# Memory operands made by ScalarE and VectorE in the neighbourhood slots instead of by GpSimd in the grouped-query ones, and fill in pieces half as long

## The chip, the cores and the metric

The kernel runs on one core of a Trainium2 chip. The metric is device time in microseconds (us) of one launch. The engines are TensorE (PE; PEld is its weight load), VectorE (DVE), ScalarE (ACT), GpSimd (POOL) and SyncE (SP), which issues nearly all DMAs. Each engine runs its instructions in the order in which the built program has them, and waits at the head of that order.

## What is computed

Two layers of an encoder over 512 tokens of width 1024, all in f32, and a final norm. One layer of the reference, cut to what matters:

```
x += W_out [ NA(h) || GQA(h) ]              h = RMSNorm(x), one input projection w_in
     NA : 8 heads, 2-D neighbourhood attention on an 8 x 64 grid, window 8 x 16, learned bias
     GQA: 8 query heads on 2 key/value heads, q and k normalised per head and rotated, 512 keys
x += MemoryCrossAttention(RMSNorm(x), RMSNorm(mem))     4 heads over 256 memory tokens
x += ConvFFN(RMSNorm(x))                    SwiGLU with a width-3 depthwise convolution

def memory_cross_attention(h, mem_n, w_q, w_kv, w_o):
    q  = (h @ w_q).reshape(b, s, MEM_HEADS, MEM_HEAD_DIM)
    kv = (mem_n @ w_kv).reshape(b, m, 2, MEM_HEADS, MEM_HEAD_DIM)
    ...
```

mem_n is RMSNorm(mem) times a gain per layer (norm_mem_kv). Its statistic does not depend on the layer; the gain does.

## The kernel before, in words

**Operands in two halves.** To keep f32 accuracy every operand of a large matmul is a pair: hi, the value cast to a shorter format (fp32r), and lo, the remainder. A product is three matmuls (mm3, L353). For weights, emit_split (L255) makes the pair: ScalarE casts (L271), GpSimd subtracts (L272). At most two raw weights and four pairs are held (N_RAW, N_W).

**Two attentions woven with filler.** In each layer the attention runs as two calls of weave (L163). The first has 8 neighbourhood units (two heads, half of the queries), the second 16 grouped-query units (two heads, a block of 128 queries). A slot of weave runs one stage of each of several units: the scores of unit s (na_scores L738, gqa_scores L907), the softmax normalisation of unit s-1 (normalise, L489, mostly on GpSimd: L490), the transposes of the probabilities of unit s-2 (na_transpose L778, gqa_transpose_p L932), and the product with the values. After a transpose, ScalarE casts the PSUM result (L483) and VectorE subtracts (L484), and only then is the PSUM buffer free. Scores use two PSUM buffers (sc), transposes and small statistics two (tr), everything else four (mm). The scores' buffers come free when ScalarE has taken the exponentials (L763, L921).

Between the stages TensorE gets other work from a Filler (L127): a chain of generators (projections of q, k, v, of the grouped-query heads, then the output projection, the memory keys and values) that yield after each piece. A Filler is asked for so many nanoseconds of matmuls (NA_FILL three times per neighbourhood slot, GQA_FILL once per grouped-query slot); it runs whole pieces until it has given them, and what it gave too much is taken off the next request. A piece is mostly 12 matmuls of 512 columns, 2.7 us. N_FIRST pieces run ahead of the first slot.

**Work that comes due later.** Late (L101) holds functions until TensorE has been given so many more LATE (3600 ns) of matmuls: late(2, double) doubles a key, late(2, straddle) copies the V blocks that straddle two tiles. The rotation of a grouped-query head is such a chain (gqa_rope, L855): swap copies (four small DMAs t<-t), a power on GpSimd (L879, 1.65 us) and a spread (L880), an addition (L884), four small matmuls with the identity ("rows"), and a split (L700, L702). PE and SP keep the program's order. For ScalarE, VectorE and GpSimd a scheduler fixes the order when the program is built, by a priority that follows the program's order; behind(n) (L193) shifts it back by n, or forward where n is negative.

**The memory operands.** memory_prepare (L523) loads mem (two DMAs of 512 KB into two r tiles) and makes, for each of 8 chunks of 128x256: a multiplication by the gain on GpSimd (L535), a cast on ScalarE (L536), a subtraction on GpSimd (L537). It is stepped in the grouped-query slots by MEM_STEPS, and the memory keys need it near the end of that stage (memory_keys, L1016). mem_stat (L545) forms the statistic once, in layer 0; its last step copies mem_rep out of a tr buffer (L570).

**Tiles.** The pool r has 22 buffers of 4 KB per partition for nearly everything in pairs, t has 12 of 2 KB for temporaries.

Of the kernel before, what the change touches and what calls it, by code (L numbers as in the profile page):

```python
# [12 lines left out]
AF = mybir.ActivationFunctionType  # L13
# [14 lines left out]
MEMN = 256  # L28
# [15 lines left out]

GQA_ORDER = ["k", 0, 1, "v", 2, 3]


NA_FILL = 2500
GQA_FILL = [2300] * 16 + [4300, 3600, 3000, 3000]
MEM_FILL = [1, 1, 2, 2, 1, 3, 1, 3, 1, 3, 1]  # L50
N_ROWS = 3
MEM_STEPS = [0, 0, 1, 0, 1, 1, 1, 1, 1, 1, 1] + [0] * 9
LATE = 3600
W_BEHIND, N_RAW, N_W, AHEAD, AHEAD_HELD, N_WARM, N_LATE, N_FIRST = 45, 2, 4, 2, 5, 8, 4, 4


class InOrder:
# [119 lines left out]
def encoder_kernel(ctx: ExitStack, tc: tile.TileContext, t: dict, out: bass.AP):  # L177
# [6 lines left out]
    cpool = ctx.enter_context(tc.tile_pool(name="cpool", bufs=1))  # L184
    xpool = ctx.enter_context(tc.tile_pool(name="xpool", bufs=1))
    wpool = ctx.enter_context(tc.tile_pool(name="wpool", bufs=N_W))
    rpool = ctx.enter_context(tc.tile_pool(name="rpool", bufs=22))
    tpool = ctx.enter_context(tc.tile_pool(name="tpool", bufs=12))
    spool = ctx.enter_context(tc.tile_pool(name="spool", bufs=24))
    psum = ctx.enter_context(tc.tile_pool(name="psum", bufs=2, space=PSUM))  # L190

# [331 lines left out]
    def memory_prepare(l):  # L523

        mops.clear()
        raw = load_mem()
        yield
        yield
        for c in range(KC):
            if c % 2 == 0:  # L530
                mg = rtile((2, 2, MEMN))
            g = par[:, l, G_MKV + c : G_MKV + c + 1]
            hi, lo = mg[:, 0, c % 2, :], mg[:, 1, c % 2, :]
            src = raw[c // 4][:, c % 4, :]
            POOL.tensor_scalar(src, src, g, 1.0, op0=ALU.mult, op1=ALU.mult)  # L535
            ACT.copy(hi, src)  # L536
            POOL.tensor_sub(lo, src, f(hi))  # L537
            mops.append((hi, lo))
            if c % 2 == 1:
                yield  # L540
# [4 lines left out]
    def mem_stat():  # L545

        acc = None
        for i in range(KC // 2):
            sq = tmp((2, MEMN))
            SP.dma_start(sq, t["memT"][i * 256 : (i + 1) * 256, :].rearrange("(k p) n -> p k n", p=P))  # L550
            yield
            ACT.activation(sq, sq, AF.Square)
            if acc is None:
                acc = sq
            else:
                POOL.tensor_add(acc, acc, sq)
        POOL.tensor_add(acc[:, 0], acc[:, 0], acc[:, 1])
        yield
        pv = ps_t()
        for b in range(MB):  # L560
            PE.matmul(pv[:, b : b + 1], acc[:, 0, b * P : (b + 1) * P], ones, start=True, stop=True)
        v = small(MB)
        DVE.tensor_scalar(v, pv[:, 0:MB], 1.0 / D, EPS, op0=ALU.mult, op1=ALU.add)
        POOL.tensor_tensor(mem_rstd, v, mhalf[:, :MB], op=ALU.pow)
        yield
        pr = ps_t()
        for b in range(MB):
            PE.matmul(pr[:, b * P : (b + 1) * P], mem_rstd[:, b : b + 1].to_broadcast([P, P]), ident,
                      start=True, stop=True)
        ACT.copy(mem_rep, pr[:, :MEMN])  # L570
        yield


# [32 lines left out]
    for l in range(DEPTH):  # L606
# [42 lines left out]
        def project_qk(n, p):  # L649
            w = get_w((n, p))  # L650
            pm = ps_mm() if p else ps_s()
            gemm_T(pm, w, xg, range(0, 4), 0, KC - 1)
            yield
            gemm_T(pm, w, xg, range(4, 8), 0, KC - 1)
            if (n, p) == ("q", 0):
                mix.stat()
                held.append(pm)
            elif (n, p) == ("k", 0):
                mix.spread()
                split_qk("q", 0, held.pop())  # L660
                split_qk("k", 0, pm)
            else:
                split_qk(n, p, pm)
            yield
# [41 lines left out]
        def project_v(g):  # L706

            w = [get_w(("v", g, kh)) for kh in range(2)]
            vs = [rtile((2, 4, P)) for _ in range(4)]
            vblk[g] = {P * b: vs[b // 2][:, b % 2] for b in range(NB)}  # L710
            vblk[g].update({P * b + 64: vs[2 + b // 2][:, b % 2] for b in range(NB - 1)})
            for b in range(NB):
                pm = ps_mm()[:, :256]
                bs = slice(b * P, b * P + P)
                for k in range(KC):
                    wh, wl = (v[:, k % 4, :] for v in w[k // 4])
                    mm3(pm, xg[k][0][:, bs], xg[k][1][:, bs], wh, wl, k == 0, k == KC - 1)
                v = vblk[g][P * b]
                split_psum(v[:, :, 0:HD], v[:, :, HD:P], pm.rearrange("p (h d) -> p h d", d=HD), mix.rstd[:, b : b + 1])
                if b == NB - 1:  # L720
                    late(2, lambda: straddle(vs))
                yield

        def straddle(vs):
# [104 lines left out]
        def gqa_project(g):  # L829
            w = get_w(("g", g))  # L830
            pm = ps_mm()
            for h in range(2):
                gemm_T(pm, w, xg, range(4 * h, 4 * h + 4), 0, KC - 1)
                if h == 0:
                    yield
            if g == "v":
                gqa_v(pm)
            else:
                gqa_rope(g, pm)
            yield  # L840
# [139 lines left out]
        def close_rows(n, ops, ready, norm, between):  # L980


            w, rows = [], []
            yield lambda: ready(1)
            for m in range(n):
                if m % 2 == 0:
                    w.append(get_w(("outg", 0, m // 2)))
                rows.append((ps_mm(), w[m // 2], slice(P * (m % 2), P * (m % 2) + P)))
                gemm_T(*rows[m][:2], ops, range(2), 0, 3, rows[m][2])
                yield  # L990
            next(between)
            yield
            yield lambda: ready(2)
            for pm, ws, c in rows:
                gemm_T(pm, ws, ops, [2], 0, 3, c)
            yield lambda: ready(3)
            yield from between
            norm = norm()

            def begin(m):  # L1000
                if m // 2 == len(w):
                    w.append(get_w(("outg", 0, m // 2)))
                rows.append((ps_mm(), w[m // 2], slice(P * (m % 2), P * (m % 2) + P)))
                gemm_T(*rows[m][:2], ops, range(3), 0, 3, rows[m][2])

            begin(n)
            for m in range(KC):
                if m == len(rows):
                    begin(m)
                pm, ws, c = rows[m]  # L1010
                gemm_T(pm, ws, ops, [3], 0, 3, c)
                norm.close(m, pm)
# [3 lines left out]
        def memory_keys():  # L1016
            yield lambda: len(mops) == KC
            for h in range(4):
                if h % 2 == 0:
                    kt = rtile((2, 2, MEMN))  # L1020
                    memk.extend((kt[:, i, 0, :], kt[:, i, 1, :]) for i in range(2))
                pm = ps_mm()[:, :MEMN]
                gemm_T(pm, get_w(("memk", h)), mops, range(KC), 0, KC - 1)
                u = tmp((MEMN,))
                DVE.tensor_mul(u, pm, mem_rep)
                ACT.copy(memk[h][0], u)
                DVE.tensor_sub(memk[h][1], u, f(memk[h][0]))
                yield

        def memory_values(g):  # L1030
# [3 lines left out]
            for b in range(MB):  # L1034
                pm = ps_mm()[:, :256]
                bs = slice(b * P, b * P + P)
                for k in range(KC):
                    wh, wl = (v[:, k % 4, :] for v in w[k // 4])
                    mm3(pm, mops[k][0][:, bs], mops[k][1][:, bs], wh, wl, k == 0, k == KC - 1)
                c = slice(256 * g, 256 * g + 256)  # L1040
                split_psum(memv[b][0][:, c], memv[b][1][:, c], pm, mem_rstd[:, b : b + 1])
                yield

        if l > 0:
# [5 lines left out]
            out_na(), memory_keys(), memory_values(0),  # L1050
            close_rows(2, PartsView(parts, 4), lambda k: whole[k], lambda: nns.append(Norm(G_MQ, l)) or nns[0],
                       memory_values(1)))
        attn_fill.step(N_FIRST if l == 0 else N_FIRST + 4)

        stat = Filler(PE, late, mem_stat()) if l == 0 else None

        def na_quanta(s):
            if l == 0 and s < 7:
                stat.step(1)
            if s == 3:  # L1060
                gtab.append(rtile((2, S), F32))
                SP.dma_start(gtab[0], t["rope"])
# [1 line left out]
            return [NA_FILL] * 3  # L1064

        weave(8, [(2, na_transpose), None, (1, na_normalise), (0, na_scores), None, (2, na_values), None], attn_fill.run, na_quanta)
        ms = Filler(PE, late, memory_prepare(l))

        def gqa_quanta(s):
            ms.step(MEM_STEPS[s])  # L1070
            return [GQA_FILL[s]]

        weave(4 * NB, [(2, gqa_transpose_p), (1, gqa_normalise), (0, gqa_scores), (3, lambda u: gqa_values(u, 0)),
                       (4, lambda u: gqa_values(u, 1)), None], attn_fill.run, gqa_quanta)
        attn_fill.finish()
        nn = nns[0]

# [328 lines left out]
```

## Time and profile before

| | |
|---|---|
| Runs | 1377.2, 1378.24, 1379.76 us; median 1378.24 |
| The profiled execution | 1377.65 us; its span 1375.1 us |
| Instructions in the span | 19228 |
| Layer 0, both attentions | about 20 to 230 us of the span: PE busy 203.87 of 210 |
| Layer 0, memory attention and FFN | 230 to 690: PE busy 458.31 of 460 |
| Layer 1, both attentions | 690 to 905: PE busy 209.09 of 215 |
| Layer 1, memory attention, FFN and end | 905 to 1375: PE busy 460.22 of 470 |
| GpSimd on the memory operands | L535 16 x 0.478 us, L537 16 x 0.742 us (median) |
| ScalarE on the memory operands | L536 16 x 0.406 us (mean) |

How to read the profile: a row of a timeline is the start, the time to the end of the last of its instructions, the engine, the line in the kernel, the operation, the tiles out<-in, the shapes and how many instructions were merged. In brackets stands how long the engine had been idle and whose work ended the wait. In a table by stretch, each engine has its busy time and its number of instructions; behind them stand the granted clock, the share of the DMA engines and GB/s. A matmul's end is modelled and reaches into the next, so PE's busy time fills some gaps.

### The profile page before, as it was taken

What the parts mean: (1) busy time and instruction counts of PE and PEld (TensorE: products, weight loads), DVE (VectorE), ACT (ScalarE), POOL (GpSimd) and SP (SyncE); (2) the same over time, 40 slices, a digit from 0 to 9 for tenths busy, and PEclk for the clock granted to TensorE, in tenths of its full rate; (3) what the DMA queues carried; (4) which work ended last, traced back from release to release, by engine and by line L of the source; (5) the groups of instructions that cost most, each with busy time, mean ns of one, the idle gap of its engine ahead of it and who ended that gap; (6) DMA issues with size and microseconds to landing.
All of it is one profiled execution on the core that took longest, in us unless ns stands there. A gap on an engine that the chain in (4) does not pass through costs nothing.

```text
span 1375.1 us, 19228 instructions
## 1 busy us (share of the span) xinstructions
PE 1348.7 (98%) x7072; PEld 1152.6 (84%) x7072; DVE 861.8 (63%) x1520; ACT 674.5 (49%) x1256; POOL 706.5 (51%) x525
## 2 busy tenths in 40 slices
PE   9999999999999999999999989999999999999997
PEld 7898789888888888888888978998788888888897
DVE  6666775565886188268546567745758834861874
ACT  6765676554543243233457657755554422432441
POOL 2557865626444443443645677657264444444441
PEclk9999999999999999999999999999999999999999
DMA  6753322222333333332266441233143333333331
GB/s 213 226 157 86 89 58 78 89 65 79 106 92 99 100 92 91 108 93 88 81 184 179 128 127 36 62 93 92 32 122 92 93 107 92 95 89 108 95 90 62
DMA packets 219293, 139.87 MB, mean 102 GB/s; under 512 B 6080, under 2 KB 212160, under 8 KB 219200
## 3 DMA queue, kind: packets, MB, share of 16 engines
q1 hardware_dynamic: 219056, 138.65, 34.4%
q8 instruction: 56, 0.92, 0.3%
q14 instruction: 37, 0.30, 0.1%
q10 hardware_dynamic: 144, 0.00, 0.0%
HBM read 126.05 MB, written 2.10 MB: 93 GB/s over the span
## 4 chain that ended last, share of the span: by engine, by line
PE 84%; DVE 5%; ACT 4%; POOL 3%; DMA 2%; issue 1%; SPq 0%; DVEq 0%; ACTq 0%; POOLq 0%
PE mm L78 75%; PE sc L78 5%; PE tr L65 3%; POOL lo L272 2%; PE tr L78 1%; ACT hi L271 1%; DVE mm L435 1%; DVE xT L436 1%; ACT t L763 1%; DMA raw<-in_w_mem_q 1%; DMA raw<-in_w_mem_o 0%; SPq L65 0%; DVE r L702 0%; DMA raw<-in_w_in 0%; ACT r L700 0%
## 5 line engine op out<-in xcount | busy, mean ns | idle before, releaser
L272 POOL TENSOR_TENSOR lo<-raw,hi 128x1024 fp32r<-128x1024 f32 (+2 forms) x268 | 498.9, 1872 | 469.8 <-ACT hi L271 467.3
L78 PE MATMUL mm<-xg,hi 128*128 128x512 f32 x1920 | 594.4, 391 | 0.7 <-ACT t L863 0.7
L78 PEld LDWEIGHTS mm<-xg,hi 128*128 128x128 f32 x1920 | 356.8, 188 | 72.6 <-ACT t L863 0.9
L271 ACT CAST hi<-raw 128x512 fp32r<-128x512 f32 (+2 forms) x276 | 224.2, 836 | 337.1 <-PE mm L78 274.7
L78 PE MATMUL mm<-xg,lo 128*128 128x512 f32 x960 | 373.8, 389 | 0.0
L78 PE MATMUL mm<-r,hi 128*128 128x512 f32 (+1 forms) x1144 | 331.5, 374 | 1.9 <-DVE xg L449 1.6
L78 PEld LDWEIGHTS mm<-r,hi 128*128 128x128 f32 x1144 | 207.0, 189 | 40.3 <-DVE xg L449 3.2
L1230 DVE SCALAR_TENSOR_TENSOR t<-t,par,t 128x7 f32<-128x7 f32 (+1 forms) x352 | 201.8, 640 | 34.0 <-ACT t L1223 34.0
L78 PE MATMUL mm<-r,lo 128*128 128x512 f32 (+1 forms) x572 | 212.9, 372 | 0.0
L78 PEld LDWEIGHTS mm<-xg,lo 128*128 128x128 f32 x960 | 180.2, 188 | 37.9
L78 PEld LDWEIGHTS mm<-r,lo 128*128 128x128 f32 x572 | 107.8, 188 | 18.7
L1215 DVE TENSOR_TENSOR t<-mm,rep 128x512 f32<-128x512 f32 x88 | 60.1, 687 | 78.2 <-PE mm L78 62.5
L490 POOL TENSOR_SCALAR t<-t,s 128x512 f32<-128x512 f32 (+1 forms) x112 | 66.7, 611 | 67.8 <-DVE s L769 32.6
L1236 DVE TENSOR_TENSOR r<-t,r 128x512 fp32r<-128x512 f32 x44 | 90.4, 2054 | 7.3 <-ACT r L1235 4.1
L1232 ACT ACTIVATE t<-t 128x512 f32<-128x512 f32 x44 | 27.9, 633 | 134.3 <-DVE t L1230 134.3
L1259 DVE TENSOR_TENSOR xT<-xT,mm 128x512 f32<-128x512 f32 x32 | 21.9, 685 | 106.8 <-PE mm L78 106.8
L65 PE MATMUL tr<-ident,t 128*128 128x128 f32 x456 | 63.0, 274 | 10.6 <-POOL t L490 4.1
L78 PE MATMUL sc<-r,r 128*128 128x256 f32 (+1 forms) x352 | 70.8, 334 | 1.8 <-ACT t L921 1.8
L65 PEld LDWEIGHTS tr<-ident,t 128*128 128x128 f32 x456 | 52.1, 141 | 21.2 <-issue 4.5
L1223 ACT ACTIVATE t<-t,par 128x512 f32<-128x512 f32 x88 | 66.8, 806 | 3.3 <-DVE t L1215 3.3
L78 PE MATMUL mm<-r,r 128*128 128x256 f32 (+1 forms) x428 | 62.6, 298 | 0.1
L78 PEld LDWEIGHTS mm<-r,r 128*128 128x128 f32 x428 | 56.1, 191 | 2.8 <-DMA r<-r 0.3
(151 smaller groups left out, 1572.0 us busy)
## 6 DMA issues: line engine op xcount, KB each, us to landing
raw<-in_w_up SPq DMA_DIRECT2D x88, 512.0 KB, 3.7
raw<-in_w_in SPq DMA_DIRECT2D x33, 512.0 KB, 4.3
raw<-in_w_down SPq DMA_DIRECT2D x32, 448.0 KB, 3.7
raw<-in_w_mem_kv SPq DMA_DIRECT2D x16, 512.0 KB, 3.8
raw<-in_w_down SPq DMA_DIRECT2D x16, 512.0 KB, 4.0
r<-in_bias SPq DMA_DIRECT2D x16, 384.0 KB, 5.5
r<-r SPq DMA_DIRECT2D x22, 256.0 KB, 4.9
raw<-in_w_out SPq DMA_DIRECT2D x8, 512.0 KB, 3.6
```

The costliest lines, as they stand in the source:

```text
L65: return lambda *a, **k: self.tc.keep_in_program_order(op(*a, **k))
L78: return self.tc.keep_in_program_order(self.engine.matmul(out, lhsT, rhs, **k))
L271: act.copy(hi[:, k], raw[:, k])
L272: (POOL if eng[0] == "P" else DVE).tensor_sub(lo[:, k], raw[:, k], f(hi)[:, k])
L435: DVE.tensor_add(pm, pm, xT[c])
L490: eng.tensor_scalar(e, e, sums[:, col : col + 1], 1.0, op0=ALU.mult, op1=ALU.mult)
L1215: DVE.tensor_mul(u, us[side], ffn.rep)
L1223: ACT.activation(cc, u, AF.Identity, bias=par[:, l, CB + ch : CB + ch + 1], scale=w[1])
L1230: DVE.scalar_tensor_tensor(cc[:, dst], u[:, src], wi, cc[:, dst], op0=ALU.mult, op1=ALU.add)
L1232: ACT.activation(cs[0], cs[0], AF.Silu)
L1236: DVE.tensor_sub(acts[j][1], cs[0], f(acts[j][0]))
L1259: DVE.tensor_add(xT[m], xT[m], pm)
```

## The change

- memory_prepare is stepped in the neighbourhood slots from slot 5 on, one step a slot, in place of the grouped-query slots; its second empty yield is gone. A chunk is now a copy with the gain as a scale on ScalarE (hi) and one scalar_tensor_tensor on VectorE, src x gain - hi (lo), both put back by 40 in the scheduler's order. GpSimd has no part in it.
- The pieces of the filler are halved: projections yield after two chunks of the contraction in place of four (6 matmuls of 512 columns), V blocks and memory values after four in place of eight, memory keys after four. N_FIRST becomes 7 and 16 (4 and 8 whole pieces before). close_rows takes two half pieces where it took one.
- NA_FILL goes from 2500 to 2550; straddle is due one LATE earlier; the copy of mem_rep is moved forward by 30.
- The pool r has 21 buffers, t 14.

```
-NA_FILL = 2500
+NA_FILL = 2550
-MEM_STEPS = [0, 0, 1, 0, 1, 1, 1, 1, 1, 1, 1] + [0] * 9
-W_BEHIND, N_RAW, N_W, AHEAD, AHEAD_HELD, N_WARM, N_LATE, N_FIRST = 45, 2, 4, 2, 5, 8, 4, 4
+W_BEHIND, N_RAW, N_W, AHEAD, AHEAD_HELD, N_WARM, N_LATE, N_FIRST = 45, 2, 4, 2, 5, 8, 4, (7, 16)
...
-    rpool = ctx.enter_context(tc.tile_pool(name="rpool", bufs=22))
-    tpool = ctx.enter_context(tc.tile_pool(name="tpool", bufs=12))
+    rpool = ctx.enter_context(tc.tile_pool(name="rpool", bufs=21))
+    tpool = ctx.enter_context(tc.tile_pool(name="tpool", bufs=14))
...
         raw = load_mem()
         yield
-        yield
         for c in range(KC):
...
-            POOL.tensor_scalar(src, src, g, 1.0, op0=ALU.mult, op1=ALU.mult)
-            ACT.copy(hi, src)
-            POOL.tensor_sub(lo, src, f(hi))
+            with behind(40):
+                ACT.activation(hi, src, AF.Copy, scale=g)
+                DVE.scalar_tensor_tensor(lo, src, g, f(hi), op0=ALU.mult, op1=ALU.subtract)
...
-        ACT.copy(mem_rep, pr[:, :MEMN])
+        with behind(-30):
+            ACT.copy(mem_rep, pr[:, :MEMN])
...
         def project_qk(n, p):
             w = get_w((n, p))
             pm = ps_mm() if p else ps_s()
-            gemm_T(pm, w, xg, range(0, 4), 0, KC - 1)
-            yield
-            gemm_T(pm, w, xg, range(4, 8), 0, KC - 1)
+            for k in range(0, KC, 2):
+                gemm_T(pm, w, xg, range(k, k + 2), 0, KC - 1)
+                if k + 2 < KC:
+                    yield
...
                     mm3(pm, xg[k][0][:, bs], xg[k][1][:, bs], wh, wl, k == 0, k == KC - 1)
+                    if k == 3:
+                        yield
...
-                    late(2, lambda: straddle(vs))
+                    late(1, lambda: straddle(vs))
...
-            for h in range(2):
-                gemm_T(pm, w, xg, range(4 * h, 4 * h + 4), 0, KC - 1)
-                if h == 0:
+            for k in range(0, KC, 2):
+                gemm_T(pm, w, xg, range(k, k + 2), 0, KC - 1)
+                if k + 2 < KC:
                     yield
...
-            next(between)
-            yield
+            for _ in range(2):
+                next(between)
+                yield
...
-                gemm_T(pm, get_w(("memk", h)), mops, range(KC), 0, KC - 1)
+                w = get_w(("memk", h))
+                gemm_T(pm, w, mops, range(0, 4), 0, KC - 1)
+                yield
+                gemm_T(pm, w, mops, range(4, 8), 0, KC - 1)
...
-        attn_fill.step(N_FIRST if l == 0 else N_FIRST + 4)
+        attn_fill.step(N_FIRST[l])
+        prepare = Filler(PE, late, memory_prepare(l))
...
         def na_quanta(s):
             if l == 0 and s < 7:
                 stat.step(1)
+            if s >= 5:
+                prepare.step(1)
...
-        ms = Filler(PE, late, memory_prepare(l))
-        def gqa_quanta(s):
-            ms.step(MEM_STEPS[s])
-            return [GQA_FILL[s]]
         weave(4 * NB, [(2, gqa_transpose_p), (1, gqa_normalise), (0, gqa_scores), (3, lambda u: gqa_values(u, 0)),
-                       (4, lambda u: gqa_values(u, 1)), None], attn_fill.run, gqa_quanta)
+                       (4, lambda u: gqa_values(u, 1)), None], attn_fill.run, lambda s: [GQA_FILL[s]])
```

More of the change, by code (lines that the diff above doesn't have):

```diff
@@ L1039, in memory_values @@
                     mm3(pm, mops[k][0][:, bs], mops[k][1][:, bs], wh, wl, k == 0, k == KC - 1)
+                    if k == 3:
+                        yield
                 c = slice(256 * g, 256 * g + 256)
```

## Prediction

> **What bounds the kernel now.** I read the page first, then busy time by stretch, then what TensorE waited for, then the engines around those waits.
>
> ```profile
> PE 1348.7 (98%) x7072; PEld 1152.6 (84%) x7072; DVE 861.8 (63%) x1520; ACT 674.5 (49%) x1256; POOL 706.5 (51%) x525
> ...
> PE   9999999999999999999999989999999999999997
> ...
> PE 84%; DVE 5%; ACT 4%; POOL 3%; DMA 2%; issue 1%; SPq 0%; DVEq 0%; ACTq 0%; POOLq 0%
> ```
>
> TensorE (PE) bounds it. The change adds and removes no matmul, so only PE's gaps can shrink. Where they are, by stretch (length, then busy time of PE, PEld, DVE, ACT, POOL):
>
> ```profile
> 60.00:145.00 85.00, 83.55 (x524) 74.52 (x523) 54.37 (x136) 53.64 (x133) 54.70 (x56) 1.00 0.46 131
> 145.00:175.00 30.00, 26.82 (x156) 22.08 (x156) 22.42 (x42) 22.06 (x52) 26.25 (x36) 1.00 0.33 98
> ...
> 690.00:808.00 118.00, 117.88 (x726) 105.36 (x725) 68.14 (x171) 71.37 (x172) 65.03 (x68) 1.00 0.51 152
> 808.00:832.00 24.00, 18.97 (x107) 15.29 (x106) 14.34 (x28) 13.08 (x28) 18.05 (x23) 1.00 0.48 139
> ```
>
> The neighbourhood stretches (60 to 145, 690 to 808) lose little; the openings of grouped-query attention (145 to 175, 808 to 832) lose 3.2 and 5.0 us, and GpSimd (POOL) is the busiest engine beside PE in the first. Busy time hides part of a gap, since matmuls overlap, so I size gaps from one matmul's start to the next, less the usual step (227 ns for 512 columns). Over 0.15 us, in layer 0: 0.36 at 85.6, 0.68 at 97.6, 0.90 at 117.1, 1.01 and 0.17 at 149 to 151, 1.79 at 159.1, 0.86 at 172.1, 0.82 and 1.00 at 218 to 220; together 7.6. In layer 1: 0.52 at 775, 1.97 at 817.7, 2.51 at 822.3, 0.17 at 825.4, 1.03 at 829.6, 0.93 at 850.8; together 7.1. So 14.7 us is the ceiling of the gain.
>
> The largest, by GpSimd's and by TensorE's instructions in order of time:
>
> ```profile
> 818.60 1.27 POOL L272 TENSOR_TENSOR lo<-raw,hi 128x512 fp32r<-128x512 f32 x1 [0.37 <-ACT hi L271]
> 819.84 1.39 POOL L535 TENSOR_SCALAR r<-r,par 128x256 f32<-128x256 f32 x3
> 821.19 1.30 POOL L272 TENSOR_TENSOR lo<-raw,hi 128x512 fp32r<-128x512 f32 x1
> 822.46 1.84 POOL L535 TENSOR_SCALAR r<-r,par 128x256 f32<-128x256 f32 x4
> 824.27 1.36 POOL L490 TENSOR_SCALAR t<-t,s 128x512 f32<-128x512 f32 x2
> ```
> ```profile
> 819.89 1.40 PE L78 MATMUL sc<-r,r 128*128 128x512 f32 x4 [1.80 <-ACT t L921]
> ...
> 825.02 1.21 PE L65 MATMUL tr<-ident,t 128*128 128x128 f32 x7 [2.35 <-POOL t L490]
> ```
>
> Seven memory multiplications (L535) stand in GpSimd's queue ahead of the softmax normalisation (L490) that the transposes need. In layer 0 the memory's casts (L536) do the same on ScalarE (ACT): they hold back the copy (L483) that frees a transpose buffer, at 159.1.
>
> ```profile
> 157.50 1.33 ACT L536 CAST r<-r 128x256 fp32r<-128x256 f32 x4
> 158.85 1.07 ACT L483 CAST xg<-tr 128x512 fp32r<-128x512 f32 x2
> ```
>
> **The change, part by part.** The order in which the built program's instructions stand on each engine is the same before and after outside the two attention stages: start, memory attention and FFN cost nothing either way, though the pools change size (r 22 to 21, t 12 to 14).
>
> GpSimd loses 16 x 0.478 (L535) and 16 x 0.742 (L537), 19.5 us. ScalarE swaps 16 casts of 0.406 for 16 scaled copies; L775, the same shape with a scale, takes 0.512, so +1.7 us. VectorE (DVE) gains 16 instructions of two SBUF operands; from L1025 with one PSUM operand (0.425) to that plus the rest of a GpSimd subtraction (L272, 1.30), so 0.43 to 1.7 each. The nearest row is L1027 (same shape, two SBUF operands): 0.415 to 0.976, median 0.818. I take 0.82, 13 us in both layers. They and the copies stand in neighbourhood slots 5 to 9, some 48 us per layer, where VectorE is 64% busy; 6.6 more make 0.78, about its share at 145 to 175 (0.75). The two memory loads go ahead of weight loads on SP's queue one slot group earlier; SP sits on its own waits there (12.8 us at 65.4), and the copies come 7 to 10 us of matmuls after the loads, which took 6.1 us to land: nothing. The wait added: the copies sit in ScalarE's in-order queue behind that load, with softmax exponentials behind them.
>
> Layer 1, opening (5.7 us of gaps). In the new order GpSimd has L272 x2 (already run at 809.0 to 811.6), then L512, L884, L879, L880, then the normalisation. From the split of the last NA output at 813.4: 1.29 + 1.29 + 1.65 + 0.61 gives 818.3, the first half normalised by 819.0; the pieces before the first transposes end at 820.2, so no wait. The first exponentials no longer stand behind ScalarE's weight cast (which caused the 1.97): 816.1 and 816.8, just before the second scores at 816.4 and 816.8. The next transposes wait for VectorE to empty their buffers behind two score maxima (0.65 each): 0.4 for the first half, 0.4 for the second, behind L977 and L873. They end at 825.9, where the trace has 831.4: **5.5 gained**. The gap at 850.8 (0.93) is a rope's split (L702 twice, 1.39) ahead of a transpose copy, with 4.1 us between transposes; there the spacing becomes 5.4 and it goes, but the previous rope's spacing falls from 5.4 to 4.1 and by the same sum gets 1.1: 0.2 lost. The wait at 775 is for a copied V block whose copy is now issued one LATE step (3.6 us of PE) earlier: 0.4 gained.
>
> Layer 0, opening (2.97 of gaps). The first transposes wait behind L879 (1.65) at 148.1, which now stands after the normalisation: 1.2 gone. L536 gone from ScalarE: 1.8 gone. But ScalarE's new order has the copies of the first transposes ahead of the second pair of exponentials (before, behind them), and the third scores need those exponentials' buffers. From the trace's own steps, transposes' start to copy 0.69, two copies 1.25, one exponential 0.70: 2.7 after their start, where 0.87 would do: 1.8 lost, and 0.5 at the fifth scores in the same way. What is late next is that. **0.7 gained.** At 172 the transposes stand one half piece (1.36) later, which covers 0.86. At 218 a slot had no fill between its transposes and the next: 2.7 us of matmuls, where emptying the first buffer took 3.6 (started 215.86, free 219.43). The halves make it 4.2: 1.8 gone, of which I take 1.5.
>
> Layer 0, neighbourhood. 97.6: mem_rep's copy no longer stands behind a weight cast (1.14): 0.5 gained. 117.1: the square waited for a temporary that PE was reading (two more bufs free it, 0.5), but its exponentials now come first and two of the new VectorE instructions stand ahead of their inputs: +0.5 to -1.1, taken as -0.3.
>
> Sum: 5.5 - 0.2 + 0.4 + 0.7 + 0.9 + 1.5 + 0.5 - 0.3 = 9.0. New waits from the fuller VectorE and ScalarE queues, which no row shows: from 0 to 16 x 0.82 = 13 if all surfaced; nearer to 0, since the stretch 60 to 145 loses under 2 us with queues at 64%; I take 1 per layer. **7.0 gained.** The profiled execution took 1377.65 (span 1375.1 and 2.55 around it), 0.6 under the runs' median of 1378.24; against the median that is **1371.2**.
>
> **A rule against it.** A VectorE operation of two SBUF operands that starts inside a GpSimd subtraction outlasts it:
>
> ```profile
> 377.92 2.41 POOL L272 TENSOR_TENSOR lo<-raw,hi 128x1024 fp32r<-128x1024 f32 x1 [4.01 <-ACT hi L271]
> ```
> ```profile
> 378.45 2.42 DVE L1236 TENSOR_TENSOR r<-t,r 128x512 fp32r<-128x512 f32 x1
> 381.44 0.69 DVE L1215 TENSOR_TENSOR t<-mm,rep 128x512 f32<-128x512 f32 x1 [0.57 <-PE mm L78]
> ```
>
> L1236 takes 0.69 alone; here 2.42, ending 0.54 after the subtraction. The Trainium skill (SBUF — State Buffer, Who interferes with whom) says that VectorE's second SBUF input comes through a port shared with GpSimd, held for a whole instruction; the row agrees. By that rule every new instruction could be held for a subtraction's rest, the upper end above.
>
> **The rivals.**
> Openings empty: the two places that I charge (ScalarE's order, 2.3; new waits, 2.0) cost nothing. For it: exponentials may come earlier than my walk has them. Against: the order is fixed. 1371.2 - 4.3 = 1366.9.
> Only the queue shortens: GpSimd's other work before the first normalisation (L272 twice, L512, L884, L879, L880) is still 7.4 us, and if it starts at 813.4 it ends at 820.8, with the rest of layer 1's gains eaten by VectorE's copies. Then about 3 us remain: 1375.2.
> Slower: the new VectorE instructions come in 8 pairs in VectorE's queue, ahead of score maxima and PSUM evictions. A pair held twice costs up to 2 x 1.3; if 1.5 surfaces on PE at each, 12 us are lost against 9.0 gained: 1381.2. It decides from 1.1 per pair. Against it: most results there are needed 5 us or more later.
> That the change does not do what it says is excluded: the 32 instructions are gone from GpSimd's order.
>
> **How the numbers follow.** The forecast 0.64 (its own range 1368 to 1375), empty openings 0.16, only the queue 0.13, slower 0.07. The range 1366.2 to 1377.0 takes in the second and third and leaves out the last. With 0.2% (2.8 us, about what a measurement of this kernel can tell from no change), faster 0.83, same 0.11, slower 0.06.
>
> **What would show it.** L535 to L537 gone from GpSimd's rows; POOL's busy time down by about 19 us; no wait over 1 us for L490 at 815 to 826; a new wait of near 1.8 us of scores for exponentials near 150; VectorE's new rows near 0.8 us; PE's gaps at 60 to 145 no larger than 2.5 us. If the new rows take 1.7 or the neighbourhood gaps reach 5 us, the forecast is wrong.

## The result and the profile after

| | before | after |
|---|---|---|
| median of the runs beside each other | 1379.65 us (1377.2 to 1379.8, 5 runs) | 1373.03 us (1372.06 to 1375.0, 5 runs) |
| the profiled execution, its span | 1377.65, 1375.1 | 1375.0, 1373.2 |

The ratio is 0.9961, 95% interval 0.9946 to 0.9975. A second set of runs of the changed kernel (the tenth experiment) gave 0.9963 (0.9950 to 0.9976). The forecast was 1371.2, inside a range of 1366.2 to 1377.0.

The page of the kernel after: busy time by engine, then the shares of the chain that ended last.

```profile
PE 1349.5 (98%) x7072; PEld 1153.9 (84%) x7072; DVE 873.0 (64%) x1536; ACT 676.9 (49%) x1256; POOL 690.0 (50%) x493
...
PE 85%; DVE 5%; ACT 3%; DMA 3%; POOL 2%; issue 1%; SPq 0%; ACTq 0%; DVEq 0%; POOLq 0%
```

GpSimd lost 32 instructions and 16.5 us, VectorE gained 16 and 11.2. The same stretches as before, with busy time of PE, PEld, DVE, ACT, POOL, then the granted clock:

```profile
60.00:145.00 85.00, 81.68 (x512) 72.48 (x512) 58.72 (x138) 55.62 (x139) 54.31 (x57) 1.00 0.48 136
145.00:175.00 30.00, 27.81 (x156) 23.10 (x155) 21.39 (x40) 19.79 (x46) 19.55 (x22) 1.00 0.22 61
690.00:808.00 118.00, 115.85 (x710) 103.58 (x709) 71.84 (x177) 74.40 (x179) 65.01 (x68) 0.99 0.57 165
808.00:832.00 24.00, 23.91 (x130) 19.93 (x130) 17.72 (x33) 14.80 (x33) 16.08 (x17) 1.00 0.24 67
```

The openings of grouped-query attention filled up (18.97 to 23.91 of 24 us in layer 1, 26.82 to 27.81 of 30 in layer 0). Both neighbourhood stretches emptied, by 1.9 and 2.0 us. So the gain was made where it was forecast, 5.9 us of busy time in the openings, and about two thirds of it, 3.9, given back in the stretches where the memory operands now stand. Whether they are the cause is a question for the experiments.

Layer 1's opening, GpSimd in order of time. The seven multiplications are gone; the normalisation (L488) runs straight behind the rope's spread (L881), and the list of what TensorE waited for has no entry from 814 to 832.

```profile
817.97 1.30 POOL L885 TENSOR_TENSOR t<-t,t 128x512 f32<-128x512 f32 x1
819.23 1.65 POOL L880 TENSOR_TENSOR s<-s,mhalf 128x8 f32<-128x8 f32 x1
820.95 0.61 POOL L881 COPY t<-s 128x512 f32<-128x512 f32 x1
821.54 1.36 POOL L488 TENSOR_SCALAR t<-t,s 128x512 f32<-128x512 f32 x2
```

Gaps are measured as in the prediction (one matmul's start to the next, less the usual step, those over 0.15 us). Before and after: 60 to 145: 1.9 and 4.1; 145 to 230: 5.6 and 3.1; layer 1's neighbourhood part: 0.5 and 3.2; its opening: 5.7 and 0.4; 832 to 905: 0.9 and 1.3. In sum 14.7 and 12.1.

The largest new gap, 2.32 us at 801, by TensorE's, ScalarE's and VectorE's rows. TensorE waits for a bank (mm) that the neighbourhood values fill and VectorE's additions (L811, L812) empty.

```profile
803.46 0.70 PE L76 MATMUL mm<-xg,hi 128*128 128x512 f32 x2 [2.15 <-DVE t L812]
```
```profile
800.23 1.14 ACT L269 CAST hi<-raw 128x512 fp32r<-128x512 f32 x2 [2.12 <-PE mm L76]
801.28 0.75 ACT L810 COPY t<-mm 64x256 f32<-64x256 f32 x2
```
```profile
801.41 0.70 DVE L895 TENSOR_TENSOR mm<-t,mm 128x512 f32<-128x512 f32 x1 [1.47 <-issue]
802.01 0.86 DVE L811 TENSOR_TENSOR t<-mm,t 64x256 f32<-64x256 f32 x2
```

The values were done near 799. ScalarE's copy of them (L810) stands behind a weight cast (L269) that idles 2.12 us until TensorE leaves the weight's buffer; VectorE's additions stand behind the multiplication of a rope's split (L895), which waits for its small matmuls. The change's new instructions beside it had ended by 799.8. In the kernel before, the copy (L809) and the additions (L810, L811) of the same values stood ahead of the next cast (L271) and of the next split (L894):

```profile
798.68 0.37 ACT L809 COPY t<-mm 64x256 f32<-64x256 f32 x1
801.07 1.14 ACT L271 CAST hi<-raw 128x512 fp32r<-128x512 f32 x2 [2.02 <-PE mm L78]
```
```profile
800.25 0.42 DVE L810 TENSOR_TENSOR t<-mm,t 64x256 f32<-64x256 f32 x1
800.70 0.42 DVE L811 TENSOR_TENSOR t<-mm,t 64x256 f32<-64x256 f32 x1
...
802.19 0.70 DVE L894 TENSOR_TENSOR mm<-t,mm 128x512 f32<-128x512 f32 x1 [0.20 <-PE mm L78]
```

Behind the gap of 2.32, some of TensorE's next steps take longer than usual, 0.9 us in sum. Such slowed steps come with a lower granted clock; the last section shows them.

### The profile page after: what moved, and what is told of

It reads as the page before. It is cut to its first block, busy times and chain, and to the rows that moved or that the text cites. A ratio compares the mean times of both kernels' runs of the same rounds, so it can differ in the third digit from the quotient of the medians.

```text
span 1373.2 us, 19230 instructions
## 1 busy us (share of the span) xinstructions
PE 1349.5 (98%) x7072; PEld 1153.9 (84%) x7072; DVE 873.0 (64%) x1536; ACT 676.9 (49%) x1256; POOL 690.0 (50%) x493
## 4 chain that ended last, share of the span: by engine, by line
PE 85%; DVE 5%; ACT 3%; DMA 3%; POOL 2%; issue 1%; SPq 0%; ACTq 0%; DVEq 0%; POOLq 0%
PE mm L76 76%; PE sc L76 5%; PE tr L63 3%; POOL lo L270 1%; PE tr L76 1%; ACT hi L269 1%; DMA t<-in_memT 1%; DVE mm L433 1%; DVE xT L434 1%; ACT t L764 1%; DMA raw<-in_w_mem_q 1%; DVE r L701 1%; DMA raw<-in_w_mem_o 0%; DMA raw<-in_w_in 0%; DVE r L482 0%
## 5 line engine op out<-in xcount | busy, mean ns | idle before, releaser
L269 ACT CAST hi<-raw 128x512 fp32r<-128x512 f32 (+2 forms) x276 | 224.1, 835 | 330.3 <-PE mm L76 272.8
L488 POOL TENSOR_SCALAR t<-t,s 128x512 f32<-128x512 f32 (+1 forms) x112 | 67.0, 614 | 73.1 <-DVE s L928 39.6
```

What stands on the lines that cost most here:

```text
L269: act.copy(hi[:, k], raw[:, k])
L488: eng.tensor_scalar(e, e, sums[:, col : col + 1], 1.0, op0=ALU.mult, op1=ALU.mult)
```

## The experiments

The gaps named below are those of each run's profile, by the same measure. The second and the eleventh run have the order of matmuls of the kernel before, the sixth one of its own; the others have the changed kernel's. The times beside a run's are those of the kernel before on the same chip.

**1. The half pieces alone.** The changed kernel with the old trio (multiplication and subtraction on GpSimd, cast on ScalarE) and MEM_STEPS back in the grouped-query slots. What else the change has (NA_FILL, N_FIRST, straddle, the pools, mem_rep's copy) stays with the half pieces here and in every run that has them in the neighbourhood stage; but for the copy, no run tells these apart.

> The pieces half as long, alone: the memory operands are made by GpSimd in the grouped-query slots as in the kernel before, all else is the changed kernel. Theory (the prediction's reasons): the gaps that the memory operands caused stay or come back, about 5 us at 808 to 832 and 1.8 in layer 0's opening; those that the halves remove are gone (the pair at 218 to 220 of 1.8, the 0.9 at 172), and the neighbourhood stretches lose no more than before, 1.9 at 60 to 145 and 2.5 at 690 to 820, since the new queue entries are missing: about 3 us below the kernel before, ratio 0.998. Rival (the neighbourhood losses of the changed kernel come from the halves themselves, which put weight casts and rope steps ahead of evictions): those stretches lose 4 and 3 or more here too, and the time is that of the kernel before or above, ratio 1.000 to 1.002.

Measured: 1379.55 against 1378.35 us, ratio 1.0007 (0.9998 to 1.0016). Neighbourhood gaps of 1.01 at 85, 1.64 at 117, 0.71 at 139 and 2.32 at 801 are all here; the two stretches lose 3.6 and 3.5. Of the changed kernel's gaps there, 0.59 at 112 alone is missing. The gaps of the kernel before at 172 and 218 are gone. The 1.97 of layer 1's scores is gone too, but the wait for GpSimd grew to 3.28:

```profile
824.18 1.84 POOL L534 TENSOR_SCALAR r<-r,par 128x256 f32<-128x256 f32 x4
825.99 1.36 POOL L489 TENSOR_SCALAR t<-t,s 128x512 f32<-128x512 f32 x2
```

The rival held: the halves bring the neighbourhood losses, and alone they gain nothing. One point fell for both: the 1.79 at 159, which the prediction put on the memory casts, is gone here, although two of the casts still stand right ahead of the transposes' copy; the gaps near it are the changed kernel's (1.57, 0.67, 0.45).

**2. The move alone.** The kernel before, with this and its stepping from slot 5 of the neighbourhood stage:

```
-            POOL.tensor_scalar(src, src, g, 1.0, op0=ALU.mult, op1=ALU.mult)
-            ACT.copy(hi, src)
-            POOL.tensor_sub(lo, src, f(hi))
+            with behind(40):
+                ACT.activation(hi, src, AF.Copy, scale=g)
+                DVE.scalar_tensor_tensor(lo, src, g, f(hi), op0=ALU.mult, op1=ALU.subtract)
```

> The memory operands moved, alone: the kernel before (whole pieces, its pools, its copy of mem_rep and its straddle step) with the operands made by ScalarE and VectorE in neighbourhood slots 5 to 9. Theory: GpSimd's queue is clear at both openings, so the 5.7 us at 808 to 832 go to about 1 and the 1.8 of layer 0 goes, while the 1.8 at 218 to 220 and the 0.9 at 172 stay; the new queue entries cost the neighbourhood stretches some 2 us each: 2 to 4 us below the kernel before, ratio 0.997 to 0.9985. Rival (the neighbourhood losses belong to the halves): the same gain in the openings with nothing lost at 60 to 145 and 690 to 808, ratio 0.995.

Measured: 1373.33 against 1378.35 us, ratio 0.9965 (0.9952 to 0.9977): the whole gain. Gone are the 2.51 and 1.03 of layer 1's opening. The 1.97 is not, for ScalarE's weight cast still stands ahead of the exponentials:

```profile
818.78 1.14 ACT L270 CAST hi<-raw 128x512 fp32r<-128x512 f32 x2 [0.51 <-PE mm L77]
819.95 0.69 ACT L919 ACTIVATE t<-sc,s 128x512 f32<-128x512 f32 x1
```

The new entries show here at one place, 1.29 at 135.9: a pair of VectorE's new instructions, 1.92 us for two that take 0.48 each where GpSimd is idle, ahead of a transpose's subtraction (L483). The ratio lies between what theory and rival gave. The gaps (3.1 at 60 to 145, where the kernel before has 1.9, and 0.4 in layer 1's neighbourhood) say that the new entries cost about one microsecond, in layer 0 alone.

**3. Two of eight chunks.** 24 of the 32 added instructions left out.

```
+            if c >= 2:
+                mops.append(mops[c % 2])
+                if c % 2 == 1:
+                    yield
+                continue
```

> The changed kernel with the operands of two of the eight chunks of memory made per layer and used for all eight, so 24 of the 32 added instructions are left out (the output is not the reference's); the order of TensorE's, GpSimd's and SyncE's instructions is the same. Theory (new waits from the fuller queues of VectorE and ScalarE cost about 4 us): the gaps at 60 to 145 and 690 to 808 fall from 4.1 and 3.2 to about 2 each, and the time lies 3 to 4 us under the changed kernel, ratio to the kernel before 0.993 to 0.994. Rival (the queues have room, the losses come from the order of older steps): within 1 us of the changed kernel, ratio 0.996.

Measured: 1373.15 us, ratio 0.9966 (0.9953 to 0.9978), as the changed kernel. Of its gaps 0.59 at 112 is missing, and 0.2 of the 0.99 at 85, a gap that differs by 0.4 between two executions of the changed kernel; 1.64, 0.71 and 2.32 stay. The rival held: the fuller queues cost 0.6 to 0.8 us, the rest of the losses comes from the order of older steps.

**4. Exponentials first.** In layer 0, the exponentials of the first three units and the copies of the first two transposes are given to ScalarE in program order.

```
+                act = ACT_IN_ORDER if l == 0 and u < 2 else ACT
                 with behind(-20):
-                    split_psum(hi, lo, tr.rearrange("p (k n) -> p k n", n=P))
+                    split_psum(hi, lo, tr.rearrange("p (k n) -> p k n", n=P), act=act)
```

> The changed kernel with ScalarE's order in layer 0's grouped-query opening turned: the exponentials of the second and third score tiles are issued ahead of the copies of the first and second transposes. Theory (the wait of scores near 152 is set by ScalarE's order): the 1.57 us start-to-start excess there goes, and that of the following scores (0.5), 1.5 to 2 us under the changed kernel, ratio 0.9945 to 0.995. Rival (the exponentials are late by VectorE's maxima, not by the order, or the values that read the later copies wait in their place): the gap moves to the values or to the next transposes and the time is that of the changed kernel.

Measured: 1374.21 us, ratio 0.9968 (0.9956 to 0.9981). The 1.57 at 152 and the 0.45 at 163.6 are gone, the 0.67 at 162 is 1.33: 1.4 us less in the stretch. The time did not follow: layer 1's opening, whose order on VectorE and GpSimd the scheduler changed too, has 1.2 where it had 0.4. So the cause of the 1.57 is shown, and its removal was worth nothing here.

**5. Two weight casts held.** An instruction can be tied behind another of its engine; the marks are the instructions named.

```
+    CAST_AFTER = {(0, ("outn", 0)): ("copy", 5), (1, ("outn", 1)): ("copy", 6)}
+    ROPE_AFTER = {(1, 0): ("add", 6)}
...
+                    with pinned(CAST_AFTER, key):
+                        act.copy(hi[:, k], raw[:, k])
...
+                with pinned(ROPE_AFTER, g):
+                    DVE.tensor_mul(pr, xr, pr)
```

> The changed kernel with two weight casts on ScalarE held until the evictions that stand behind them are issued (layer 0: the cast for the first output weight behind the sixth value copy; layer 1: the cast for the second output weight behind the seventh value copy), and one rope split on VectorE in layer 1 held behind the same unit's value additions. TensorE's order is unchanged. Theory (the neighbourhood losses that the half pieces brought come from ScalarE's in-order queue: a weight cast that waits for TensorE to leave its buffer stands ahead of the copies that free TensorE's next output bank): the excess of 1.64 at 117.6 falls to 0.4 or less and that of 2.32 at 801 to 0.4 or less, with the slowed steps after it gone: 3 to 4.5 us under the changed kernel, ratio to the kernel before 0.993 to 0.994. Rival (the output banks would be freed as late by VectorE, or the later cast makes the weights late): the two gaps keep over half their size or come back within 10 us, and the ratio stays at 0.996.

Measured: 1371.11 against 1379.38 us, ratio 0.9945 (0.9932 to 0.9959). The 1.64 is 0.55, the 2.32 is 0.53, no slowed steps follow. ScalarE near 117 in the changed kernel, where the square (L864) stands behind the cast and four exponentials, and in this run, where it (L872) stands ahead of the cast:

```profile
115.85 1.14 ACT L269 CAST hi<-raw 128x512 fp32r<-128x512 f32 x2 [2.80 <-PE mm L76]
...
118.70 0.61 ACT L864 ACTIVATE t<-mm 128x512 f32<-128x512 f32 x1
```
```profile
117.18 0.61 ACT L872 ACTIVATE t<-mm 128x512 f32<-128x512 f32 x1
117.81 0.76 ACT L818 COPY t<-mm 64x256 f32<-64x256 f32 x2
118.60 1.14 ACT L277 CAST hi<-raw 128x512 fp32r<-128x512 f32 x2
```

And VectorE near 801, with the additions (L819, L820) ahead of the split (L904):

```profile
798.82 0.86 DVE L819 TENSOR_TENSOR t<-mm,t 64x256 f32<-64x256 f32 x2
799.71 0.42 DVE L820 TENSOR_TENSOR t<-mm,t 64x256 f32<-64x256 f32 x1
...
801.20 0.70 DVE L904 TENSOR_TENSOR mm<-t,mm 128x512 f32<-128x512 f32 x1
```

The theory held in its mechanism: what stands ahead of the evictions in the two in-order queues made these gaps. It fell short in size, for both gaps were to be 0.4 or less and the ratio 0.993 to 0.994. At 801 the cast and the split were held together, so their shares aren't told apart. The gaps at 85, 112, 139 and 895 weren't touched by the edit.

**6. The move, with half pieces only in the late fill, and other casts held.** Whole pieces for projections; memory keys, values and close_rows as in the change; mem_rep's copy forward.

```
+    CAST_AFTER = {(0, ("outn", 0)): ("copy", 5), (1, ("outn", 2)): ("exp", 0)}
```

> The operands moved, whole pieces in the neighbourhood stage, half pieces only in the memory keys and values and between the first output rows, mem_rep's copy put forward as in the change, and two weight casts held (the first output weight's in layer 0 behind the sixth value copy, the third's in layer 1 behind the first exponentials). Theory (the operands' move brings the gain, the half pieces pay only at 218 to 220, and the 1.97 of layer 1's second scores is a weight cast ahead of the exponentials): against the run with the operands alone, 1.8 gone at 218 to 220, 1.6 gone at 818, 0.5 at 97 and up to 0.9 at 117: 4 to 5 us less, about 1368.5 to 1369.5, ratio 0.993. Rival (a gap taken away there reappears at the next step, as it did with the exponentials put first): within 1.5 us of the run with the operands alone, ratio 0.9955 to 0.9965.

Measured: 1374.17 us, ratio 0.9964 (0.9952 to 0.9977). The 1.82 at 218 is gone and the 1.97 is 0.32, so its cause was the cast. But 0.61 and 0.96 appear at the next transposes (waits for the normalisation and for VectorE), and 0.68 at 98 and 0.90 at 118 stayed, so the held cast was not their cause. At 98 the rows show another weight cast (97.47 to 98.61), and mem_rep's copy still stands behind it (98.63), although it is put forward as in the change: putting it forward is not what frees it. The rival held.

**7 and 8. Who and when.** The old trio, but in the neighbourhood slots (7); ScalarE and VectorE, but in the grouped-query slots (8). Both with the half pieces.

> The changed kernel, with the memory operands made in the same neighbourhood slots but by the old trio, multiplication and subtraction on GpSimd and the cast on ScalarE. Theory (the place in time is what pays, GpSimd has room in the neighbourhood slots: 64% busy and 9.8 us of work added per layer over some 48 us): the openings at 145 to 175 and 808 to 832 stay as in the changed kernel, and the neighbourhood stretches lose 0 to 2 us more: ratio 0.9955 to 0.9975. Rival (the engine is what pays: normalisations there wait behind seven multiplications in GpSimd's queue as they did in the openings): waits of over 1 us for the normalisation's transposes at 95 to 135 and 765 to 805, 5 us or more in sum, ratio 0.9995 to 1.002.

Measured: 1378.18 against 1379.38 us, ratio 0.9997 (0.9987 to 1.0007). The openings are as in the changed kernel. The neighbourhood lost 7.0 in layer 0 (3.11 at 117.7, and the slowed steps behind it) and 4.0 in layer 1. The time is the rival's, its mechanism is not: the profile shows no wait for a normalisation there; the long one is for ScalarE's square (L864, at 120.32). It starts when VectorE is through with the rope's products (L862, L863) and a reciprocal (L770), and the products follow another rope multiplication (L895) here; in the changed kernel they ran ahead of it, at 116.14.

```profile
118.22 0.70 DVE L895 TENSOR_TENSOR mm<-t,mm 128x512 f32<-128x512 f32 x1 [1.99 <-ACT t L764]
118.82 0.75 DVE L862 SCALAR_TENSOR_TENSOR t<-mm,qkg,r 128x512 f32<-128x512 f32 x1
```

> The changed kernel, with the memory operands made by ScalarE and VectorE but in the grouped-query slots where GpSimd made them before. Theory (both matter: GpSimd's queue is clear, so the 2.5 to 3.3 us of transposes for normalisations near 823 go, but ScalarE's scaled copies and VectorE's subtractions now stand among exponentials, maxima and transpose copies, with VectorE at 0.75 in those stretches): about half of the gain, ratio 0.997 to 0.9985. Rival 1 (only the engine matters): the openings as in the changed kernel, ratio 0.9955 to 0.9965. Rival 2 (only the place in time matters): the openings lose as before, 5 us at 808 to 832, ratio 0.9995 to 1.001.

Measured: 1382.38 us, ratio 1.0028 (1.0017 to 1.0038): slower than the kernel before, which none of the three expected. ScalarE's scaled copy stands at the head of its queue until the memory has landed, with the exponentials behind it that the next scores need:

```profile
821.90 0.91 ACT L535 ACTIVATE r<-r,par 128x256 fp32r<-128x256 f32 x2 [3.24 <-DMA r<-in_memT]
822.83 0.69 ACT L924 ACTIVATE t<-sc,s 128x512 f32<-128x512 f32 x1
```
```profile
823.66 1.86 PE L77 MATMUL sc<-r,r 128*128 128x512 f32 x4 [3.85 <-ACT t L924]
```

So neither half of the move pays alone, beside half pieces. In the opening ScalarE cannot take a wait for a load. In the neighbourhood slots the trio cost what the openings gained, in layer 0 by another order of older steps on VectorE (1.5 us more at 117.7) and the slowed steps behind it (1.6 us); how its entries brought that order about isn't shown.

**9. The fifth run with the exponentials first as well.**

> The changed kernel with the two weight casts and the rope split held as in the run that held them, and also with layer 0's second and third exponential pairs ahead of the copies of the first and second transposes on ScalarE; layer 1's order is not touched by it this time. Theory (with the exponentials first, the 1.57 near 151 and the 0.45 near 162 go and the 0.67 near 161 grows to 1.33, as the run with that edit alone showed; what that run lost in layer 1 came from a side effect on layer 1's order): 1.3 us under the run with the casts held, about 1369.8, ratio 0.9935. Rival (the gap moves to a later step of the same opening): the same time as the run with the casts held, ratio 0.9945.

Measured: 1371.0 against 1379.23 us, ratio 0.9939 (0.9925 to 0.9953). The gaps at 145 to 230 fall from 3.1 to 1.8, as expected, and layer 1's opening keeps its 0.4. Against the fifth run the times can't tell them apart. Beside the changed kernel on the same chip it is 3.5 us less.

**10 and 11. Both kernels again.**

> The changed kernel itself once more, on the same chip as the run that holds the casts and turns the exponentials, for the spread of its gaps between executions. Theory: the gaps at 85, 112, 117.6, 139, 152, 162, 210, 801, 838 and 895 come back at the same places with the same size to 0.3 us, since they are set by the order of the queues, and what differs between executions is the start (0 to 60) and the slowed steps after long gaps: 1373 us, ratio 0.996. Rival (the gaps of the first profile were that execution's accident): other places and sizes, by a microsecond or more.

Measured: 1374.55 us, ratio 0.9963 (0.9950 to 0.9976). All gaps come back where they were, to 0.1 us except the one at 85 (1.41). After the 2.32 at 802 no step is slowed this time.

> The kernel before itself once more, for the spread of its gaps between executions. The sum of PE's start-to-start excess explains 2 us of the difference between the two profiled executions, where the medians differ by 4 to 7. Theory (the long wait of 2.5 us at 822 is followed in some executions by some eight slowed matmul steps, as the 3.3 us wait of the run with the half pieces alone was): the same gaps at the same places, and up to 1.5 us more of slowed steps at 825 to 830 and in the start, a span of 1376 to 1378. Rival (other gaps than those of the first profile appear): new places with over 0.5 us.

Measured: 1378.58 (1377.95 to 1383.18) against 1379.68 us, ratio 0.9992 (0.9977 to 1.0007). The same gaps at the same places; this time 1.3 us of slowed steps follow the 2.55 at 821.6, and none are in the start. Profile against profile the change brought 1.9 to 2.8 us (spans 1375.1 and 1375.5, 1373.2 and 1372.7), the ratios say 3.4 to 7.4. The mean granted clock of the runs of the kernel before was 0.993 to 0.997, of the changed one 0.995 to 0.998, 0.001 to 0.002 between their medians; if all of that is slowed steps, it is 1.4 to 2.8 us of 1375 (an estimate). Two more things bear on the rest. Time and span differ by 2.0 to 2.6 us in the runs of the kernel before, by 1.8 in the changed kernel's: 0.6 us of the gain lies outside the span, which the trace doesn't cover, and the first run, which gained nothing, has it too. And the profile of the eleventh run is of the fastest of its eight runs, the first profile after of the slowest of its five. What else the other executions hold isn't traced and stays open.

## Why the prediction was right, and where it was not

Each term against the gaps of the first profile after:

| term | forecast | measured |
|---|---|---|
| layer 1's opening | +5.5 | 5.68 to 0.40: +5.3 |
| the gap at 850.8 | -0.2 | 0.93 to 0.85, at 838: +0.1 |
| straddle, 775 | +0.4 | 0.51 to 0: +0.5 |
| layer 0's opening | +0.7 | 2.97 to 2.69: +0.3 |
| 172 | +0.9 | 0.86 to 0: +0.9 |
| 218 to 220 | +1.5 | 1.82 to 0.44, at 210: +1.4 |
| mem_rep, 97.6 | +0.5 | 0.68 to 0.19: +0.5 |
| 117.1 | -0.3 | 0.90 to 1.64: -0.7 |
| new waits | -2.0 | -5.6 |

The first eight sum to 8.3, where 9.0 was forecast. With the last, 2.7 us are left, where 7.0 was forecast and the medians show 6.6. So that the time came within 2 us of the forecast is in part luck: the last term was 3.6 too small, and 3.9 us of the measured gain stand in no term of the sum (0.6 of it outside the span, see the eleventh run; the rest is open).

The failed step is the last term, "New waits from the fuller VectorE and ScalarE queues": 0.6 more at 85, 0.59 at 112, 0.71 at 139, 2.32 at 801 with 0.9 of slowed steps behind it, 0.41 at 895, in sum 5.6 where 2.0 was charged. It was mis-sized, and its reason was wrong: the third run took most of the new instructions out of those queues and got 0.8 us at most. The first run has nearly all of it without them. The half pieces, and what goes with them, make it, by changing which weight cast or rope split ScalarE and VectorE have ahead of an eviction; the fifth run shows that for 117 and 801, for 85, 139 and 895 it is argued. The prediction charged such orders in the openings and 0.3 at 117.1 (0.7 came, in the first run too, without the new instructions); for the other neighbourhood gaps it priced the new instructions alone.

Of its own signs, these held: L535 to L537 are gone from GpSimd, no transposes of the opening wait for a normalisation, scores wait 1.57 near 150. Two did not: GpSimd's busy time fell by 16.5 us and not by 19, and the gaps at 60 to 145 are 4.1, where it allowed 2.5. With layer 1's 3.2 the neighbourhood gaps are 7.3, and it had called itself wrong from 5.

In the openings it read the order rightly. Its 5.5 for layer 1 is a difference of end times; by its own gaps, with two waits of 0.4 left of 5.7, it would be 4.9. The two came as 0.19 and 0.21. In layer 0 the forecast wait of 1.8 for the exponentials came as 1.57 (ScalarE's idle time, then the copies, then the exponentials):

```profile
151.94 1.07 ACT L481 CAST xg<-tr 128x512 fp32r<-128x512 f32 x2 [3.73 <-PE tr L63]
152.90 0.70 ACT L922 ACTIVATE t<-sc,s 128x512 f32<-128x512 f32 x1
```
```profile
153.75 1.40 PE L76 MATMUL sc<-r,r 128*128 128x512 f32 x4 [1.41 <-ACT t L922]
```

Three credits went to the wrong part of the change. "L536 gone from ScalarE: 1.8 gone" happens with the halves alone, while the move alone leaves 0.47 and 0.73 of it. The 0.68 at 97.6 is 0.19 with the halves, but stays with the copy put forward and whole pieces (sixth run). And of layer 1's 5.3 the move takes 3.7, while the 1.97 leaves with the halves, which shift the weight cast. The move alone is still worth the whole gain, since the halves give back what they take.

The new VectorE instructions were priced well: 16 took 12.7 us, where 13 were forecast. One of the long ones, by VectorE's row and by GpSimd's, and the line's summary (least, median and most ns):

```profile
785.14 1.45 DVE L534 SCALAR_TENSOR_TENSOR r<-r,par,r 128x256 fp32r<-128x256 f32 x1
```
```profile
783.68 2.63 POOL L270 TENSOR_TENSOR lo<-raw,hi 128x512 fp32r<-128x512 f32 x2
```
```profile
L534 DVE SCALAR_TENSOR_TENSOR r<-r,par,r x16: 472/588/1497, 95.8 to 799.3; 128x256 fp32r<-128x256 f32 x16
```

The eight that found GpSimd idle, or began before its instruction, took 0.47 to 0.49; this one began inside a subtraction that ended at 786.31 and ended 0.28 after it, and all eight that began inside such an operation of GpSimd ended 0.28 to 0.29 after it. The Trainium skill (SBUF — State Buffer, Who interferes with whom) says that a VectorE instruction with two SBUF inputs contends with a GpSimd instruction that reads SBUF, and the rows agree. The rival built on it, 1.5 us surfacing at each of eight pairs, did not come; it came at one place, in the second and the sixth run, for 1.3.

"Empty openings" fell with the 1.57. "Only the queue shortens" (1375.2) had the wrong place: layer 1's opening gave nearly all it had, and the loss was in the neighbourhood stretches.

## What to carry to other kernels

When work leaves a queue, look for what else stands ahead of the waiting instruction in each in-order queue; a prefetch (a weight cast that waits for its buffer) ahead of an eviction is a wait for the eviction too. Resizing filler can change those orders anywhere, as it did here, so it has a cost of its own to be looked for, apart from what it covers. Ask of moved work both who does it and when: here the one alone gained nothing (0.9997), the other lost (1.0028), and both together, in the changed kernel, gave 0.9961.

## What the runs showed of the hardware

A long wait of TensorE can cost more than itself. In the seventh run the wait of 2.9 us is followed by a stretch at half the granted clock (the third number from the end), in which steps of 512 columns take 0.43 us in place of 0.23:

```profile
112.00:117.60 5.60, 5.19 (x38) 4.67 (x37) 2.96 (x11) 1.69 (x6) 5.60 (x6) 1.00 0.46 138
117.60:121.00 3.40, 0.46 (x5) 0.26 (x4) 2.09 (x4) 2.02 (x8) 3.30 (x5) 0.98 0.06 15
121.00:124.00 3.00, 3.00 (x7) 2.42 (x8) 1.67 (x4) 1.19 (x3) 1.19 (x3) 0.50 0.45 97
124.00:128.00 4.00, 4.00 (x26) 3.50 (x26) 0.67 (x2) 1.12 (x3) 2.31 (x2) 0.97 0.33 115
```

Seven steps lose 0.2 to 0.4 each here, 1.6 us in sum; behind the other two gaps of over 3 us it is 1.3 and 1.7. Half clock followed all gaps of 3.1 us and more (3.11, 3.28, 4.01), and some of those from 2.3 to 2.6: the gap of 2.3 near 801 stands in seven profiles, and three of them paid 0.8 to 1.0 behind it, the other four nothing. The changed kernel is in both groups. In the start it followed shorter waits in some executions: in the first profile of the kernel before, the granted clock is 0.50 from 8.0 to 10.8, behind gaps of 1.23 and 0.56. The Trainium skill (TensorE: Matmul & The Clock Gate, HAM oscillation — how this bites in real kernels) warns of idle gaps above about 3.4 us; here the half clock also followed a gap of 2.3 (idle for 2.15), so the measurement decides.
